# Stick-breaking output by partial summation: suffix products times value differences in place of sigmoid times suffix product

## The chip, the cores and the metric

The program is one inference step of a two-layer encoder trunk. It runs on one core of a Trainium2 chip, as one launch. Such a core has five engines that run side by side, each through its own list of instructions in order: TensorE (PE in the profile, with its weight loads as PEld), VectorE (DVE), ScalarE (ACT), GpSimd (POOL) and SyncE (SP), the last two of which issue most of the DMA transfers here. They wait for each other by semaphores. The metric is the time of the whole launch in microseconds (us): median 2755.19 us of three runs (2753.42 to 2755.53).

## The reference: what is computed

The change touches one thing, the stick-breaking attention of layer 0 for the prompt: 1024 positions, 8 heads of 64 columns, blocks of 128 queries.

```python
def stick_breaking(q, k, v, q_pos, k_pos):
    z = jnp.einsum('bqhd,bkhd->bhqk', q, k).astype(jnp.float32) * (HEAD_DIM ** -0.5)
    mask = k_pos[None, :] < q_pos[:, None]
    log_keep = jnp.where(mask, jax.nn.log_sigmoid(-z), 0.0)
    between = lax.cumsum(log_keep, axis=3, reverse=True) - log_keep
    w = jnp.where(mask, jnp.exp(jax.nn.log_sigmoid(z) + between), 0.0)
    return jnp.einsum('bhqk,bkhd->bqhd', w.astype(v.dtype), v)
```

With keep_k = sigmoid(-z_k) (1 where masked), the weight of key j is sigmoid(z_j) times the product of keep_k over all later keys k > j. Write S_j for the product of keep_k over k >= j. Since sigmoid(z_j) = 1 - keep_j, the weight is also S_{j+1} - S_j, with S_n = 1 behind the last key.

Beside the prompt, layer 0 computes the same for 8 sample streams of 16 queries against 1024 cached and 16 new keys, and a convolution module (31 taps, depthwise, 512 channels) in parallel. An output projection, a squared-ReLU MLP, a second layer with chunk-band attention and a second MLP follow.

## The kernel before

Layer 0's mixer is the function `mixer0`; in the trace it fills the first 545 us or so. Tokens stand along the free dimension, channels on the 128 partitions: 1152 tokens (`T`), 1024 of them prompt (`TP`). The 8 heads go by pairs `p` = 0 to 3, two heads `i` to a pair. Per pair, five lists of steps are merged: the prompt's attention (`attend`), the sample attention, the projections of the next pair (`proj(p+1)`) and, for pairs 0 and 1, the gate and value projections of two further convolution channel blocks (`ag`). The merge goes by the PE time of each step. Into this list come the convolution's taps (`tap`, one DVE operation over 1024 columns and one over 128 for each of 31 taps of each of 4 channel blocks), spread by their DVE cost: 26 ahead of pair 0, then 36, 38 and 24 in pairs 0, 1 and 2. In pair 3 the place of the projections is taken by the first part of the output projection (`psoa`), the convolution's normalisation (`conv_norm`) and the reload of finished pieces from DRAM (`cr`). The program's recording layer then fixes the order of each engine's own list, which can differ from the order of the code by some places.

One head's attention goes in four jobs `t` of two query blocks (`q` = 2t, 2t+1). For a block of n = 128(q+1) keys:

- PE makes the logits z (names `z`, lines 924 to 927), 512 columns to a bank.
- ACT takes sigmoid(z) into `w` (tile `sg`, line 928) and sigmoid(-z) into `keep` (tile `kp`, line 929).
- DVE runs `stick`: a scan from the right that turns `keep` into suffix products (line 907), then w[j] times keep[j+1] (line 909).
- PE transposes w block by block (`tpa`, line 388), ACT copies the transposed blocks out (`wa`, line 390), PE multiplies them by the transposed values `vs` (`ava`, line 398), two half-results on partitions 0 to 63 and 64 to 127 of one bank.
- `finish`: ACT copies one half out (`ata`, line 406), DVE adds the other (`cpa`, line 410), and POOL stores the piece in DRAM (`cat_d`, line 363).

The values of a pair arrive from the projection as tile `sv` (channels by tokens). POOL stores that tile as an output (`out_sb_v`, line 881). `expand_v` transposes it on PE in three groups (`vt`, line 898), and ACT copies the result into `vs` (line 900) and, for the sample's new keys, into `vn` (line 903). The sample attention calls the same `stick` from `soft`, with tiles `sgs` and `kps`.

Tiles with one tag share buffers: `sg` has three, `kp` two, `sv` and `vs` one each.

Of the kernel before, what the change touches and what calls it, by code (L numbers as in the profile page):

```python
# [8 lines left out]
F32 = mybir.dt.float32  # L9
F32R = mybir.dt.float32r  # L10
AF = mybir.ActivationFunctionType
ALU = mybir.AluOpType
# [3 lines left out]
P = 128  # L16
# [3 lines left out]
TP = 1024  # L20
# [104 lines left out]
def tile_trunk(ctx, tc, ins, outs):  # L125
    nc = tc.nc
    ACT = nc.scalar.activation
    tt = nc.vector.tensor_tensor
# [5 lines left out]
    def pool(name):  # L134
        return tc.tile_pool(name=name, bufs=1, reuse_waits="tile")
# [7 lines left out]
    def bank(name):  # L143
        return psum.tile([P, 512], F32, tag="ps", name=name)
# [225 lines left out]
                split(hi, lo, piece[rows, at - c0:at - c0 + m])  # L370
                at += m

    def weigh_steps(vs, wk, cat, i, t, blocks, name, scored):


        order = sorted(blocks.keys, key=lambda j: -len(blocks.keys[j]))
        groups = []
        for two in zip(order[::2], order[1::2]):
            n, m = (P * len(blocks.keys[j]) for j in two)
            groups.append(([(two[0], 0, n), (two[1], n, m)], n + m))  # L380
        st = {"w": {}}

        def turn(gi):
            items, used = groups[gi]
            tp = bank(f"tp{name}{gi}")
            for j, c0, n in items:
                for q, tile_q in enumerate(blocks.keys[j]):
                    nc.tensor.transpose(tp[:, c0 + q * P:c0 + (q + 1) * P], blocks.get(j, tile_q), ident)
            st["w"][gi] = wk.tile([P, 512], F32, tag="wt", name=f"w{name}{gi}")
            ACT(st["w"][gi][:, :used], tp[:, :used], AF.Copy)  # L390

        def prod(gi):

            if gi == 0:
                st["av"] = bank(f"av{name}")
            for m, (j, c0, n) in enumerate(groups[gi][0]):
                o0 = 0 if 2 * t in blocks.keys[j] else P
                mm(st["av"][64 * m:64 * m + 64, o0:o0 + n], vs[:, j, i], st["w"][gi][:, c0:c0 + n], start=gi == 0,
                   stop=gi == last)

        def finish():
            own = slice(64 * i, 64 * i + 64)
            av = st["av"]
            one = P if t == 0 else 0
            tmp = wk.tile([P, 256], F32, tag="av", name=f"at{name}")
            ACT(tmp[own, one:], av[64:128, one:256], AF.Copy)
            piece = wk.tile([P, 256], F32, tag="cat", name=f"cp{name}")
            if one:
                ACT(piece[own, :one], av[0:64, :one], AF.Copy)
            prior["weights"] = tt(piece[own, one:], av[0:64, one:256], tmp[own, one:], ALU.add)  # L410
            cat.put(piece, own, t * 256, 256)

        def pcost(gi):
            return 4 * groups[gi][0][0][2] * PASS

        def tcost(gi):
            return groups[gi][1] / P * 109

        last = len(groups) - 1
        def turns(gi):  # L420
            return Step(tcost(gi), lambda: turn(gi), 0.0, f"turn{name}{gi}", None if gi else scored, 4500)

        lag = 4500 if cat.layer == 0 else 2500

        def prods():
            for gi in range(last + 1):
                prod(gi)
            finish()


        return ([turns(gi) for gi in range(last + 1)]
                + [Step(sum(pcost(gi) for gi in range(last + 1)), prods, 330.0, f"out{name}", f"turn{name}{last}", lag)])
# [222 lines left out]
    def mixer0():  # L655
        with ExitStack() as st:

            ep = Bufs(st.enter_context(pool("early0")), sg=3, kp=2)
# [3 lines left out]
            maskd = ep.tile([P, P], F32R, "maskd", "maskd")  # L662
            unit = ep.tile([P, P], F32R, "unit", "unit")
            rp = Bufs(st.enter_context(pool("rstd0")), rv=3)
            pp = Bufs(st.enter_context(pool("pair0")))
            wk = Bufs(st.enter_context(pool("work0")), wt=4, wts=1, cat=2)
            S = {"qb": qb}

# [216 lines left out]
            def expand_qk(p):  # L885
# [4 lines left out]
                ACT(S["qn"], q[:, TP:], AF.Copy, scale=0.125)  # L890
                ACT(S["kn"], k[:, TP:], AF.Copy)

            def expand_v(p, g):
                v = S["sv", p]
                tp = bank(f"vt0{p}{g}")
                for i in range(3):
                    c = (3 * g + i) * P
                    nc.tensor.transpose(tp[:, i * P:(i + 1) * P], v[:, c:c + P], ident)
                n = 3 if g < 2 else 2
                ACT(vs[:, 3 * g:3 * g + n], tp[:, :n * P].rearrange("p (j h d) -> p j h d", j=n, h=2), AF.Copy)  # L900
                if g == 2:
                    S["vn"] = pp.tile([P, P], F32, "vn", f"vn0{p}")
                    ACT(S["vn"], tp[:, 2 * P:3 * P], AF.Copy)

            def stick(w, keep, n):

                nc.vector.tensor_tensor_scan(keep[:, 0:n][:, ::-1], keep[:, 0:n][:, ::-1],  # L907
                                             ones[:, 0:1].to_broadcast([P, n]), 1.0, ALU.mult, ALU.mult)
                tt(w[:, 0:n - 1], w[:, 0:n - 1], keep[:, 1:n], ALU.mult)

            def attend(p, cat):
                def job(i, t):
                    ws = {}

                    def one(q):
                        n = (q + 1) * P
                        w = ep.tile([P, TP], F32, "sg", f"sg{p}{i}{q}")
                        keep = ep.tile([P, TP + P], F32, "kp", f"kp{p}{i}{q}")
                        qc = slice(q * P, q * P + P)
                        for c in range(0, n, 512):  # L920
                            m = min(512, n - c)
                            z = bank(f"z{p}{i}{q}{c}")
                            last = c + m == n
                            mm(z[:, :m], qs[i][:, qc], kd[i][:, c:c + m], start=True, stop=False)
                            mm(z[:, :m], qs[i][:, qc], kl[i][:, c:c + m], start=False, stop=not last)
                            if last:
                                mm(z[:, m - P:m], unit, maskd, start=False, stop=True)
                            ACT(w[:, c:c + m], z[:, :m], AF.Sigmoid)
                            ACT(keep[:, c:c + m], z[:, :m], AF.Sigmoid, scale=-1.0)
                        stick(w, keep, n)  # L930
                        ws[q] = w

                    keys = {j: [q for q in (2 * t, 2 * t + 1) if j <= q] for j in range(2 * t + 2)}
                    blocks = Blocks(keys, lambda j, q: ws[q][:, j * P:(j + 1) * P])
                    q0, q1 = 2 * t, 2 * t + 1

                    def cost(q):
                        return 2 * max(256, q * P + P) * PASS

                    def dcost(q):  # L940
                        return 2 * (60 + (q * P + P) / 0.96)

                    name = f"a{p}{i}{t}"
                    return (Step(cost(q0), lambda: one(q0), dcost(q0)),
                            Step(cost(q1), lambda: one(q1), dcost(q1), f"z{name}"),
                            weigh_steps(vs, wk, cat, i, t, blocks, name, f"z{name}"))

                return [job(i, t) for i in range(2) for t in range(4)]

            def soft(bg, z, zn, s):  # L950
                tt(zn[:, 0:P], zn[:, 0:P], masks[:, 0, 64 - 64 * bg:192 - 64 * bg], ALU.add)
                w = wk.tile([P, TP + P], F32, "sgs", f"sgs{s['p']}{bg}")
                keep = ep.tile([P, TP + P], F32, "kp", f"kps{s['p']}{bg}")
                for src, c, n in ((zn, TP, P), (z[1], 512, 512), (z[0], 0, 512)):
                    ACT(w[:, c:c + n], src[:, :n], AF.Sigmoid)
                    ACT(keep[:, c:c + n], src[:, :n], AF.Sigmoid, scale=-1.0)
                stick(w, keep, TP + P)
                s["w"] = w

            start()  # L960
# [1 line left out]
            vs = pp.tile([P, 8, 2, HD], F32, "vs", "vs0")  # L962
# [3 lines left out]
            for p in range(4):  # L966
                S["p"] = p
                expand_qk(p)
                if p < 3:
# [3 lines left out]
                    n = TAPS[p + 1]  # L973
# [8 lines left out]
                cat = Cat(0, p, wk, cat_t)  # L982
                jobs = attend(p, cat)
                body, left = pipeline(jobs[1:], jobs[0][2])
                steps = carry + [jobs[0][0]] + [Step(327.0, lambda p=p, g=g: expand_v(p, g)) for g in range(NG)]
                if p == 3:
                    late, = ready_chunks(0, [2], pp, cat_t)
# [750 lines left out]
    class Next:  # L1738
# [48 lines left out]
        def run_rows(self, g):  # L1787
            self.rows[g]()

    cat = mixer0()  # L1790
    rst = Bufs(ctx.enter_context(pool("rstd")), rv=3)
    with pool("mlp0") as mp_:
# [39 lines left out]
    cat = mixer1(n1, win)  # L1832
# [134 lines left out]
```

## Time and profile before

| what | us |
|---|---|
| median of three runs | 2755.19 |
| lowest, highest | 2753.42, 2755.53 |
| span of the profiled execution, first to last instruction | 2748.2 |
| PE busy in it | 2669.0 |
| DVE busy in it | 2090.5 |
| ACT busy in it | 1389.0 |

The profile is of one execution; it has a span of its own, 7.0 us below the median of the timed runs. The page lists for each engine how long it was busy, cuts the span in 40 slices, follows the chain of waits back from the last instruction, and groups instructions by line, operation and tile: the count, the sum of the busy time (overlaps counted once), the mean of one in ns, and the idle time before them with what ended it. Other views used below are tables by stretch of time, lists of one engine's instructions in order of time with the idle time before each in square brackets, and totals of who waited for whom. Matmuls overlap in the pipeline and their ends are modelled, so a busy PE is not PE at its peak; PE's idle time is the sure part.

### The profile page before, as it was taken

How to read it: one execution, taken by the hardware profiler on the slowest of the kernel's cores; microseconds unless marked ns; L12 is line 12 of the kernel's file. 1: busy time of each engine (PE TensorE's matmuls, PEld its weight loads, DVE VectorE, ACT ScalarE, POOL GpSimd, SP SyncE). 2: the span in 40 equal slices, each digit the busy share in tenths (PEclk: the TensorE clock that was granted, in tenths of full speed). 3: DMA queues.
4: the chain of work that ended last, by engine and by line, in shares of the span. 5: the costliest groups of instructions: out<-in, count | busy, mean ns of one | idle time of the engine just before them, and what ended most of it. 6: DMA issues, size and time to landing. Idle time of an engine off the chain costs nothing.

```text
span 2748.2 us, 50583 instructions
## 1 busy us (share of the span) xinstructions
PE 2669.0 (97%) x19362; PEld 2557.1 (93%) x19362; DVE 2090.5 (76%) x4117; ACT 1389.0 (51%) x2906; POOL 328.3 (12%) x599
## 2 busy tenths in 40 slices
PE   8999898999999999999999999998999999999998
PEld 8987776799999999999999999997999999999998
DVE  8999998888777755758577777778787777647577
ACT  5344456755554543435355555556555555434344
POOL 1100101041111100000011111110221111100001
PEclk9999999999999999999999999999999999999999
DMA  4434446454343377435444444446533343684344
GB/s 157 121 111 147 118 141 223 145 176 143 139 146 141 138 260 250 124 100 170 146 140 138 140 135 135 139 132 229 179 132 137 141 145 138 230 270 134 96 125 145
DMA packets 173203, 422.90 MB, mean 154 GB/s; under 512 B 25968, under 2 KB 53808, under 8 KB 170912
## 3 DMA queue, kind: packets, MB, share of 16 engines
q1 hardware_dynamic: 135696, 288.38, 33.1%
q0 software_dynamic: 37120, 131.27, 13.9%
q8 instruction: 152, 2.49, 0.4%
q14 instruction: 91, 0.75, 0.1%
q10 hardware_dynamic: 144, 0.02, 0.0%
HBM read 289.60 MB, written 117.34 MB: 148 GB/s over the span
## 4 chain that ended last, share of the span: by engine, by line
PE 76%; DVE 12%; ACT 4%; issue 4%; DMA 3%; POOL 0%; SPq 0%; DVEq 0%; ACTq 0%; POOLq 0%
PE um L1461 25%; PE pd L1686 25%; PE psc L225 10%; PE psp L225 3%; DVE y L735 3%; PE avc L467 2%; PE tpc L455 2%; DVE kp L907 2%; PE f L225 1%; PE psoa L225 1%; DMA cr<-cat_d 1%; PE zc L1201 1%; PE zc L1202 1%; PE zs L568 1%; PE so L602 1%
## 5 line engine op out<-in xcount | busy, mean ns | idle before, releaser
L225 PE MATMUL psc<-h,hl_wc 128*128 128x384 f32 x1728 | 327.2, 339 | 0.0
L225 PEld LDWEIGHTS psc<-h,hl_wc 128*128 128x128 f32 x1728 | 296.8, 188 | 13.3 <-issue 10.9
L1461 PE MATMUL um<-sl,hl_m 128*128 128x288 f32 x1548 | 240.3, 295 | 0.0
L1461 PEld LDWEIGHTS um<-sl,hl_m 128*128 128x128 f32 x1548 | 217.7, 188 | 0.0
L1686 PE MATMUL pd<-tm,hl_wd 128*128 128x288 f32 x1584 | 214.7, 294 | 0.0
L1686 PEld LDWEIGHTS pd<-tm,hl_wd 128*128 128x128 f32 x1584 | 211.3, 189 | 0.0
L735 DVE SCALAR_TENSOR_TENSOR y<-u,dw,y 128x1024 f32<-128x1024 f32 (+1 forms) x232 | 177.8, 806 | 0.6
L225 PE MATMUL psp<-h,hl_wi 128*128 128x384 f32 x864 | 165.7, 344 | 0.0
L1468 ACT ACTIVATE hdm<-hdm 128x288 f32<-128x288 f32 x192 | 84.7, 442 | 156.5 <-DVE hdm L1467 154.8
L225 PEld LDWEIGHTS psp<-h,hl_wi 128*128 128x128 f32 x864 | 150.9, 191 | 7.0 <-issue 6.2
L186 DVE TENSOR_TENSOR tm<-xr,tm 128x576 fp32r<-128x576 f32 (+1 forms) x120 | 85.8, 715 | 93.9 <-ACT tm L185 93.6
L185 ACT ACTIVATE tm<-xr 128x576 fp32r<-128x576 f32 (+1 forms) x120 | 77.6, 646 | 95.8 <-PE pd L1686 74.0
L1168 ACT ACTIVATE s<-s,mxc 128x640 f32<-128x640 f32 (+4 forms) x128 | 88.9, 694 | 60.2 <-DVE mxc L1165 58.6
L1461 PE MATMUL um<-sl,hl 128*128 128x288 f32 x756 | 119.1, 296 | 0.0
L1686 PE MATMUL pd<-th,hl_wd 128*128 128x288 f32 x792 | 113.7, 297 | 3.8 <-DVE th L186 3.7
L1686 PEld LDWEIGHTS pd<-th,hl_wd 128*128 128x128 f32 x792 | 108.2, 190 | 4.8 <-DVE th L186 4.2
L1686 PE MATMUL pd<-xr,hl_wd 128*128 128x288 f32 x792 | 112.4, 296 | 0.0
L1686 PEld LDWEIGHTS pd<-xr,hl_wd 128*128 128x128 f32 x792 | 108.0, 190 | 0.0
L1461 PEld LDWEIGHTS um<-sl,hl 128*128 128x128 f32 x756 | 106.4, 188 | 0.8
L1686 PE MATMUL pd<-tm,hl 128*128 128x288 f32 x768 | 104.9, 295 | 0.0
L1686 PEld LDWEIGHTS pd<-tm,hl 128*128 128x128 f32 x768 | 103.1, 188 | 0.0
L185 ACT ACTIVATE whc<-tpc 128x512 fp32r<-128x512 f32 (+1 forms) x144 | 72.5, 523 | 46.7 <-PE tpc L455 45.8
(526 smaller groups left out, 6637.0 us busy)
## 6 DMA issues: line engine op xcount, KB each, us to landing
xr<-hb_d SPq DMA_DIRECT2D x208, 288.0 KB, 3.0
xr<-in_w_up_dram SPq DMA_DIRECT2D x64, 512.0 KB, 4.2
hb_d<-hdm POOLq DMA_DIRECT2D x96, 288.0 KB, 2.4
hb_d<-t POOLq DMA_DIRECT2D x96, 288.0 KB, 2.4
wm<-in_w_down_dram SPq DMA_DIRECT2D x64, 256.0 KB, 4.0
st_wd<-in_w_down_dram SPq DMA_DIRECT2D x64, 256.0 KB, 3.5
st_wc<-in_w_in_c_dram SPq DMA_DIRECT2D x44, 256.0 KB, 2.9
xm_d<-xo POOLq DMA_DIRECT2D x16, 576.0 KB, 3.5
```

The source lines that it names most:

```text
L185: ACT(hi, src, AF.Copy)
L186: return tt(lo, src, f(hi), ALU.subtract)
L225: mm(ps()[:, :G], hl[:, a, at:at + P], act[g][k // 4][b][:, k % 4, :], start=n == 0, stop=n == len(todo) - 1)
L455: nc.tensor.transpose(tp[:, c0 + q * P:c0 + (q + 1) * P], blocks.get(j, tile_q), ident)
L467: mm(st["av"][:, o0:o0 + n], vs[:, j, i].rearrange("p a d -> p (a d)"), src[:, c0:c0 + n], start=st["done"] == 0, stop=st["done"] == nmm - 1)
L568: mm(box["z"][at // 512][own, at % 512:at % 512 + kw], qb[:, own], k[:, b * kw:b * kw + kw], start=True, stop=True)
L735: stt(src if j == CW - 1 else dst, src, wj, dst, ALU.mult, ALU.add)
L907: nc.vector.tensor_tensor_scan(keep[:, 0:n][:, ::-1], keep[:, 0:n][:, ::-1], ones[:, 0:1].to_broadcast([P, n]), 1.0, ALU.mult, ALU.mult)
L1168: ACT(s[:, :n], s[:, :n], AF.Exp, bias=mx, scale=-1.0, accum_out=tot)
L1461: mm(banks[b, n][:, :TQ], w[:, a, c * P:c * P + P], combo(key, c)[:, h, n * TQ:n * TQ + TQ], start=k < 3 and c == 0 and i == 0, stop=c == ...
L1468: ACT(y, y, AF.Relu)
L1686: mm(ps, w[:, a, m * P:m * P + P], b[:, h, (n - ns[0]) * TQ:(n - ns[0]) * TQ + TQ], start=first and s == 0, stop=j == NJ - 1 and s == 2, s ...
```

## The change

`stick` keeps the scan and loses the product. For the prompt, only sigmoid(-z) is taken, into tile `sg`; its suffix products S go straight to the transposes. The values are replaced by differences: column j of `sv` becomes v[j-1] - v[j], column 0 becomes -v[0] (the new function `differences`, called ahead of the transposes of each pair, once the values have been sent to the output). Then the sum over j of S_j (v[j-1] - v[j]) plus the value of the block's last key is the output. That last value, for the 8 query blocks of a head, is copied ahead into a small tile `ve`, on both halves of the partitions, and comes in as the bias of the copy in `finish`, which is made once per query block since each has a bias of its own. The sample attention keeps both sigmoids and the product, which moves from `stick` into `soft`.

```diff
-    def weigh_steps(vs, wk, cat, i, t, blocks, name, scored):
+    def weigh_steps(vs, ends, wk, cat, i, t, blocks, name, scored):
...
             tmp = wk.tile([P, 256], F32, tag="av", name=f"at{name}")
-            ACT(tmp[own, one:], av[64:128, one:256], AF.Copy)
             piece = wk.tile([P, 256], F32, tag="cat", name=f"cp{name}")
-            if one:
-                ACT(piece[own, :one], av[0:64, :one], AF.Copy)
+
+            for e in range(2):
+                cols = slice(e * P, e * P + P)
+                dst, rows = (piece, slice(0, 64)) if one and e == 0 else (tmp, slice(64, 128))
+                ACT(dst[own, cols], av[rows, cols], AF.Identity, bias=ends()[rows, i, 2 * t + e:2 * t + e + 1])
             prior["weights"] = tt(piece[own, one:], av[0:64, one:256], tmp[own, one:], ALU.add)
...
-            pp = Bufs(st.enter_context(pool("pair0")))
+            pp = Bufs(st.enter_context(pool("pair0")), ve=2)
...
+            def differences(p):
+
+
+                v = S["sv", p]
+                ends = S["ends", p] = pp.tile([P, 2, 8], F32, "ve", f"ve{p}")
+                for i in range(2):
+                    for rows in (slice(0, 64), slice(64, 128)):
+                        ACT(ends[rows, i], v[64 * i:64 * i + 64, P - 1:TP:P], AF.Copy)
+                tt(v[:, 1:TP][:, ::-1], v[:, 0:TP - 1][:, ::-1], v[:, 1:TP][:, ::-1], ALU.subtract)
+                ACT(v[:, 0:1], v[:, 0:1], AF.Copy, scale=-1.0)
+
             def expand_v(p, g):
                 v = S["sv", p]
+                if g == 0:
+                    differences(p)
...
-            def stick(w, keep, n):
+            def stick(keep, n):
 
                 nc.vector.tensor_tensor_scan(keep[:, 0:n][:, ::-1], keep[:, 0:n][:, ::-1],
                                              ones[:, 0:1].to_broadcast([P, n]), 1.0, ALU.mult, ALU.mult)
-                tt(w[:, 0:n - 1], w[:, 0:n - 1], keep[:, 1:n], ALU.mult)
...
-                        w = ep.tile([P, TP], F32, "sg", f"sg{p}{i}{q}")
-                        keep = ep.tile([P, TP + P], F32, "kp", f"kp{p}{i}{q}")
+                        keep = ep.tile([P, TP], F32, "sg", f"sg{p}{i}{q}")
...
-                            ACT(w[:, c:c + m], z[:, :m], AF.Sigmoid)
                             ACT(keep[:, c:c + m], z[:, :m], AF.Sigmoid, scale=-1.0)
-                        stick(w, keep, n)
-                        ws[q] = w
+                        stick(keep, n)
+                        ws[q] = keep
...
-                stick(w, keep, TP + P)
+                stick(keep, TP + P)
+                tt(w[:, 0:TP + P - 1], w[:, 0:TP + P - 1], keep[:, 1:TP + P], ALU.mult)
```

The order of the engines' lists moves with it at three places that matter below. In these lists the number behind a name is its buffer, and the scan is listed as SCALAR_TENSOR_TENSOR with `ones` as input. Lines 735, 877, 907, 924 and 925 of before are 737, 879, 922, 937 and 938 of the changed kernel.

First, DVE at the start of pair 0, behind the first block's scan (`y` are convolution taps). Before:

```order
L907 SCALAR_TENSOR_TENSOR kp_1099<-kp_1099,ones 128x128
L735 SCALAR_TENSOR_TENSOR y_771<-u_382,dw,y_771 128x1024
L909 TENSOR_TENSOR sg_1098<-sg_1098,kp_1099 128x127
L735 SCALAR_TENSOR_TENSOR y_771<-u_382,dw,y_771 128x1024
L735 SCALAR_TENSOR_TENSOR y_771<-u_382,dw,y_771 128x128
L735 SCALAR_TENSOR_TENSOR y_771<-u_382,dw,y_771 128x1024
L877 TENSOR_TENSOR sq_1178<-psp_1108,rh_315 128x384
```

and of the changed kernel, at the same place:

```order
L922 SCALAR_TENSOR_TENSOR sg_1098<-sg_1098,ones 128x128
L737 SCALAR_TENSOR_TENSOR y_771<-u_382,dw,y_771 128x1024
L737 SCALAR_TENSOR_TENSOR y_771<-u_382,dw,y_771 128x128
L737 SCALAR_TENSOR_TENSOR y_771<-u_382,dw,y_771 128x1024
L903 TENSOR_TENSOR sv_1003<-sv_1003 128x1023
L737 SCALAR_TENSOR_TENSOR y_771<-u_382,dw,y_771 128x1024
L879 TENSOR_TENSOR sq_1179<-psp_1105,rh_315 128x384
```

The product is gone, and three tap operations behind the scan stands the difference of the values, which waits for the transfer of `sv` to the output.

Second, PE at the same time (`psp` is the next pair's projection, `vt` the transposes of the values). Before, the transposes stood between the halves of a group of the projection:

```order
L225 MATMUL psp_1108<-h_30_171,hl_wi_0_966 128x384
L898 MATMUL vt_1121<-ident,sv_1003 128x128 x3
L898 MATMUL vt_1128<-ident,sv_1003 128x128 x3
L898 MATMUL vt_1133<-ident,sv_1003 128x128 x3
L568 MATMUL zs_1140<-ct00k_1142,qb_124 32x256 x4
L225 MATMUL psp_1108<-h_40_178,hl_wi_1_971 128x384
```

Now they stand behind the second half, ahead of the second block's logits:

```order
L225 MATMUL psp_1105<-h_70_190,hl_wi_1_971 128x384
L913 MATMUL vt_1125<-ident,sv_1003 128x128 x3
L913 MATMUL vt_1132<-ident,sv_1003 128x128 x3
L913 MATMUL vt_1137<-ident,sv_1003 128x128 x3
L570 MATMUL zs_1144<-ct00k_1146,qb_124 32x256 x4
L937 MATMUL z_1173<-k_743,q_741 128x256
```

They moved down by 12 matmuls of 384 columns, and behind them PE can do nothing else while they wait.

Third, DVE at the end of pair 0, where the last block's weights are made while pair 1 is prepared (`l` and `q` are the split keys and queries of the next pair, `u` the last tap). Before:

```order
L735 SCALAR_TENSOR_TENSOR u_389<-u_389,dw,y_1239 128x1024
L735 SCALAR_TENSOR_TENSOR u_389<-u_389,dw,y_1239 128x8x16
L351 TENSOR_TENSOR l_745<-sk_1870,k_743 64x1024
L907 SCALAR_TENSOR_TENSOR kp_2126<-kp_2126,ones 128x1024
L351 TENSOR_TENSOR l_746<-sk_1870,k_744 64x1024
L909 TENSOR_TENSOR sg_2125<-sg_2125,kp_2126 128x1023
```

Now:

```order
L737 SCALAR_TENSOR_TENSOR u_389<-u_389,dw,y_1237 128x1024
L922 SCALAR_TENSOR_TENSOR sg_2084<-sg_2084,ones 128x1024
L737 SCALAR_TENSOR_TENSOR u_389<-u_389,dw,y_1237 128x8x16
L351 TENSOR_TENSOR l_746<-sk_1840,k_744 64x1024
L353 SCALAR_TENSOR_TENSOR q_742<-sq_1179,q_742 64x1024
```

The scan, now the last step ahead of PE's transposes, stands ahead of the split keys instead of between them. In pairs 1 and 2 the differences stand among the next convolution block's taps, more than 20 operations behind DVE's last part of the values; in pair 3 they stand 17 behind it, after the split of the first reloaded piece.

More of the change, by code (lines that the diff above doesn't have):

```diff
@@ L945, in job @@
                             Step(cost(q1), lambda: one(q1), dcost(q1), f"z{name}"),
[L946 removed]
+                            weigh_steps(vs, lambda: S["ends", p], wk, cat, i, t, blocks, name, f"z{name}"))
                 return [job(i, t) for i in range(2) for t in range(4)]
```

## Prediction

> **What bounds the kernel now.** I first asked which engine is full where the changed work stands. A table by stretches of the trace, with the attention's pairs 0 to 2 in the first (100 to 425 us), the change to pair 3 in the second and pair 3 in the third, gives per stretch its length and each engine's busy time with its count, then the clock and the DMA engines:
>
> ```profile
> core 0: us, PE busy (x) PEld busy (x) DVE busy (x) ACT busy (x) POOL busy (x), PEclk, DMA share, GB/s
> 225.00:250.00 25.00, 25.00 (x176) 20.51 (x174) 23.33 (x35) 10.59 (x28) 0.54 (x1) 1.00 0.41 128
> 275.00:300.00 25.00, 22.46 (x173) 19.50 (x172) 22.85 (x33) 11.15 (x29) 2.50 (x4) 1.00 0.28 72
> 100.00:425.00 325.00, 305.26 (x2276) 261.34 (x2274) 316.97 (x418) 160.78 (x376) 31.61 (x56) 0.98 0.44 132
> 425.00:445.00 20.00, 12.53 (x64) 7.84 (x65) 10.84 (x18) 6.89 (x15) 4.88 (x10) 0.83 0.90 303
> 445.00:550.00 105.00, 98.44 (x718) 78.96 (x715) 94.17 (x177) 84.84 (x186) 8.69 (x16) 0.98 0.51 172
> ```
>
> From 100 to 425 us DVE is busy 316.97 of 325 (97.5%), PE 305.26. Two engines are nearly full, and PE's 19.7 us of idle time are all that can certainly be had while PE's work stays as it is. Whom it waits for is told by the totals of PE's waits in that stretch (us in total, times, longest):
>
> ```profile
> PE tpa L388 <- DVE sg L909: 16.1, 7, 6.2
> PE z L924 <- DVE u L715: 1.0, 1, 1.0
> PE tpa L388 <- DVE cpa L410: 0.8, 1, 0.8
> PE z L924 <- DVE sk L877: 0.7, 1, 0.7
> ```
>
> 18.6 of the 19.7 us are waits for DVE, 16.1 of them of the transposes for the very product that goes. So DVE decides here, though PE looks full. How DVE comes to be late is seen at the longest wait, in DVE's and PE's lists in order of time (start, duration; idle time before it in brackets):
>
> ```profile
> 205.32 5.91 DVE L735 SCALAR_TENSOR_TENSOR y<-u,dw,y 128x128 f32<-128x128 f32 x8
> ...
> 214.47 2.27 DVE L907 TENSOR_TENSOR_SCAN kp<-kp,ones 128x1024 f32<-128x1024 f32 x1
> 216.78 1.22 DVE L351 TENSOR_TENSOR l<-sk,k 64x1024 fp32r<-64x1024 f32 x1
> 218.03 1.23 DVE L909 TENSOR_TENSOR sg<-sg,kp 128x1023 f32<-128x1023 f32 x1
> 219.31 0.90 PE L388 MATMUL tpa<-ident,sg 128*128 128x128 f32 x3 [6.17 <-DVE sg L909]
> ```
>
> PE stops at 213.1. DVE works on without a gap, taps first, starts the last block's scan 1.3 us later and ends its product at 219.3: a backlog, not one slow operation. Such a wait costs twice. The table of PE in steps of 2 us (busy time, then the granted clock) shows the clock at half from 216 to 222 us, past the wait's end:
>
> ```profile
> 212.00:214.00 2.00, 1.14 (x7) 1.00 0.00 0
> 214.00:216.00 2.00, 0.00 (x0) 0.80 0.65 262
> ...
> 220.00:222.00 2.00, 2.00 (x8) 0.50 0.66 128
> 222.00:224.00 2.00, 2.00 (x20) 0.99 0.91 218
> ```
>
> From 219.3 to 222 PE worked at half speed, which lost 1.35 us more.
>
> **The change part by part.** The groups that go, and the nearest rows for what is added:
>
> ```profile
> L909 DVE TENSOR_TENSOR sg<-sg,kp 128x127 f32<-128x127 f32 (+3 forms) x64 | 47.9, 749 | 0.6
> L928 ACT ACTIVATE sg<-z 128x512 f32<-128x512 f32 (+2 forms) x96 | 47.8, 498 | 19.8 <-PE z L927 10.1 <-PE tpa L388 4.6 <-PE z L925 4.1
> L406 ACT ACTIVATE ata<-ava 64x256 f32<-64x256 f32 (+1 forms) x32 | 11.3, 354 | 41.1 <-PE ava L398 40.7
> L1041 ACT ACTIVATE yl<-yl,cvec 128x384 f32<-128x384 f32 x12 | 8.2, 697 | 0.1
> L1773 ACT ACTIVATE sqh<-x 128x384 f32<-128x384 f32 x21 | 9.6, 512 | 0.7 <-DVE accs L1774 0.5
> ```
>
> *DVE.* 64 products go, 47.9 us. Four subtractions of 128x1023 come; their row is the product of that size, 1.23 us at 218.03: 4.9 us. Net 43.0, of which pairs 0 to 2 hold three quarters, 32.3. DVE's work in the first stretch falls to 284.7 us.
>
> *ACT.* 96 sigmoids go, 47.8 us. The copies of `finish` become two of 128 columns with a bias, in place of one of 256. An operation of 128x384 with two operands read per partition took 697 ns against 512 without (L1041, L1773), so about 0.09 us for one; 0.27 us is the shortest L406 copy, of 128 columns. That makes 2 x 0.36 in place of 0.38, or +0.34 us for each of 24 jobs and +0.18 for each of 8: 9.6 us. The four copies of last values and the sign change cost at most 5 x 0.27 per pair, 5.4. Net 33 us less. ACT is busy half of the first stretch, so I count none of this as gain; the 0.34 us in `finish` lie under other PE work, and without that cover would be 32 x 0.34 = 11 us at most.
>
> *PE* does the same matmuls.
>
> *What follows for PE, pairs 0 to 2.* The 18.6 us of waits for DVE shrink but needn't vanish: DVE's 284.7 us will stand in about 309, still 92%. The table's slices where DVE is as busy today, 225 to 250 (93%) and 275 to 300 (91%), have 0 and 2.54 us of PE idle. That bounds the rest by 0 and 309/25 x 2.54 = 31, which is more than today; between such ends I go by the longest waits, which are a backlog of 3 to 6 us built up over 100 us of stretch, when a pair now frees 10.8 us of DVE. I leave 5.0 us. Gain 13.6, and 1.35 for the clock.
>
> *The new wait.* `sv` may be overwritten only when its store has landed; then DVE subtracts, ACT changes a sign, and PE transposes. In pair 0 there is no distance:
>
> ```profile
> 106.97 0.56 POOL L881 DMA_DIRECT2D out_sb_v_dram<-sv  x1 [3.93 <-ACT sv L879]
> out_sb_v_dram<-sv POOLq DMA_DIRECT2D x1, 576.0 KB, 4.0
> out_sb_v_dram<-sv POOLq DMA_DIRECT2D x1, 576.0 KB, 9.2
> 106.27 2.34 PE L225 MATMUL psp<-h,hl_wi 128*128 128x384 f32 x12
> 108.44 1.15 PE L898 MATMUL vt<-ident,sv 128*128 128x128 f32 x9
> 108.99 0.41 DVE L907 TENSOR_TENSOR_SCAN kp<-kp,ones 128x128 f32<-128x128 f32 x1
> 109.32 1.25 DVE L735 SCALAR_TENSOR_TENSOR y<-u,dw,y 128x1024 f32<-128x1024 f32 x1
> ```
>
> The store is issued at 107.0 and took 4.0 us to land (pair 0; 9.2 in pair 3): 111.0. DVE's list puts a scan and three tap operations from 109.0 ahead of the subtraction, to 112.0. Plus 1.23 and some 0.4 for ACT and two signals: 113.6. PE, with 12 more matmuls ahead (2.1 us), is there at 110.5. So PE stands 3.1 us, and behind its transposes queue all later logits and projections; DVE fills its own time with taps. For a clock that may drop in it I add 0.7, half of the 1.35 above. In pairs 1 to 3 the subtraction stands 17 or more DVE operations behind the last of the values, and PE's transposes later still: nothing, as long as a store lands within about 10 us. Cost 3.8.
>
> [...]
>
> *Into pair 3.* The chain of waits goes through reloaded pieces (`cr`), the first of which may start when DVE has split the last keys (line 351):
>
> ```profile
> 419.08 1.05 ACT L348 ACTIVATE k<-sk 64x1024 fp32r<-64x1024 f32 x1 [0.17 <-PE z L924]
> 423.56 1.22 DVE L351 TENSOR_TENSOR l<-sk,k 64x1024 fp32r<-64x1024 f32 x1
> 424.81 7.86 DMA cr<-cat_d
> 434.77 6.57 DMA cr<-cat_d
> ```
>
> The keys were ready at 420.1, DVE came at 423.56. PE idles 7.5 us from 425 to 445, but two transfers of 7.86 and 6.57 us stand in a row behind that split, so this stretch gains only DVE's lateness: 3.4.
>
> *Pair 3.* PE's waits there for DVE or for a `keep` tile, from the totals of 445 to 550:
>
> ```profile
> PE sn L582 <- DVE cpa L410: 1.2, 1, 1.2
> PE st L588 <- ACT kp L929: 1.0, 1, 1.0
> PE z L924 <- DVE cs L638: 0.7, 1, 0.7
> PE st L588 <- DVE xo L1086: 0.7, 1, 0.7
> PE tpa L388 <- DVE xo L1086: 0.4, 1, 0.4
> ```
>
> Together 4.0 us. Here no subtraction is left to pay, and 12 us of DVE's 94 go; I count them whole. Behind 550 us nothing is touched.
>
> *Sum.* 13.6 + 1.35 - 3.8 + 3.4 + 4.0 = 18.5 us. The profiled span goes from 2748.2 to 2729.7. The timed median lies 7.0 us above the span; carried over, 2755.2 - 18.5 = **2737 us**.
>
> **The rivals.** *Waits stay (2747).* In-order lists, taps first: the backlog forms again, 13 us of the 18.6 stay, and the gain in pair 3 halves. 5.6 + 1.35 - 3.8 + 3.4 + 2.0 = 8.5 us. For it speaks the slice with 91% and 2.5 us idle; against it that 16.1 us hang on the removed product itself.
>
> *DVE sets the pace outright (2721).* PE's busy time is partly modelled; its weight loads are busy only 261.34 of 325 us. If PE has hidden room, the first stretch shortens by DVE's whole 32.3 us less the 3.8: 28.5, with 3.4 and part of pair 3 (2.5) 34.4. Against it: PE's list shows nearly unbroken matmuls, and small ones need little loading. [...]
>
> *Nothing to be seen (2754).* Residual waits of 15 us and half the gain behind: 3.6 + 1.35 - 3.8 + 0 = about 1.
>
> *Slower (2768).* The wait for the store, in every pair. DVE's list is in order: should the store land late (9.2 us instead of 4.0 would move 113.6 to 117.8), DVE, the sign change on ACT and all of PE stand behind it. 7.3 us and 1.4 of clock per pair make 34.8; without any such wait the gain would be 22.3, so 12.5 lost. It decides from 22.3/4 = 5.6 us per pair. Against it: the distance in pairs 1 to 3.
>
> **How the numbers follow.** Forecast 0.54, waits stay 0.17, DVE's pace 0.11, nothing 0.11, slower 0.07. Two runs of this kernel can't tell less than 0.2% (5.5 us) from no change: faster is the first three, 0.82, same 0.11, slower 0.07. The forecast's own range is 2731 to 2744 (residual waits of 0 to 11 us give 2732 to 2743, pair 0's wait of 0 to 7 gives 2733 to 2741, one at a time). To leave out no more than 2 in 10 the range takes in the stay of waits and most of DVE's pace: 2721 to 2752.
>
> **What would show it.** Right: no wait of `tpa` above 2 us between 100 and 425, DVE's share there near 92%, a wait of `vt` of about 3 us near 110, the first `cr` earlier by more than the rest, the later stages unchanged in length. Wrong: PE's waits of the same total on another DVE row (`cpa`, `u`), waits for `sv` in pairs 1 to 3, or a stretch that shortens by more than PE's idle time.

## The result, and the profile after

The changed kernel takes 2728.57 us (median of four runs, 2724.97 to 2731.01) against 2754.31 us before (four runs, 2749.01 to 2755.53): ratio 0.991, 95% interval 0.9896 to 0.9924. The forecast was 2737 us, faster. The profiled execution spans 2727.3 us, 20.9 us less than that of before.

To see where the 20.9 us lie, both traces are cut at the same events: the first transposes of the values (`vt`) of pairs 0, 1, 2 and 3, and the first `psob` matmul (second part of the output projection), which ends pair 3. The fifth row is everything from the first MLP on. The columns are the stretch and its length, each engine's busy time (operations), the mean granted clock, the DMA share and GB/s. Before:

```profile
core 0: us, PE busy (x) PEld busy (x) DVE busy (x) ACT busy (x) POOL busy (x), PEclk, DMA share, GB/s
108.44:234.33 125.89, 117.58 (x866) 100.94 (x865) 121.91 (x164) 56.05 (x128) 12.23 (x22) 0.97 0.48 143
234.33:349.03 114.70, 107.75 (x795) 92.11 (x795) 111.79 (x150) 55.45 (x130) 10.98 (x19) 0.99 0.42 127
349.03:447.13 98.10, 86.15 (x653) 68.85 (x653) 87.39 (x116) 55.39 (x132) 12.21 (x22) 0.95 0.49 157
447.13:542.66 95.53, 89.09 (x658) 71.10 (x657) 86.17 (x161) 77.31 (x170) 8.69 (x16) 0.98 0.53 182
605.83:2748.20 2142.37, 2106.58 (x15495) 2065.23 (x15494) 1536.99 (x3272) 1055.89 (x2180) 244.94 (x458) 1.00 0.48 155
```

After:

```profile
111.32:226.97 115.65, 113.51 (x854) 97.83 (x854) 109.10 (x144) 50.37 (x116) 12.45 (x22) 1.00 0.49 147
226.97:333.96 106.99, 105.35 (x794) 90.87 (x794) 102.34 (x135) 48.93 (x117) 11.43 (x19) 1.00 0.44 137
333.96:425.67 91.71, 84.39 (x651) 67.83 (x652) 77.81 (x102) 50.11 (x120) 12.23 (x22) 0.94 0.53 167
425.67:518.27 92.60, 86.97 (x658) 69.64 (x657) 76.09 (x144) 70.08 (x150) 8.68 (x16) 1.00 0.56 188
581.83:2727.30 2145.47, 2109.58 (x15495) 2068.16 (x15494) 1536.49 (x3272) 1056.39 (x2181) 245.73 (x458) 0.99 0.46 155
```

Pairs 0 to 3 are shorter by 10.2, 7.7, 6.4 and 2.9 us. Their start is 2.9 us later, the output projection 0.4 and the rest of the program 3.1 us longer. The 3.1 us are not the change's: the trace's records of the granted clock show 27.2 us at half speed there against 20.8 before, on the same instructions. Nor is it the change's that PE's first logits (`z`), behind the same 528 matmuls, start at 103.75 us instead of 105.98: of these 2.2 us up to 1.7 (half of 3.41) are a half speed from 51.4 to 54.8 us, which of the two only the trace of before has. In pair 0, 12 matmuls (866 less 854) are not saved but moved ahead of the cut, some 2.1 us.

The waits of PE from 100 to 409 us (us in total, times, longest), pairs 0 to 2 of the changed kernel, answer to the totals shown of before, where `tpa` for `sg` alone had 16.1 us, longest 6.2:

```profile
PE vt L913 <- ACT sv L904: 4.6, 2, 2.9
PE tpa L388 <- DVE sg L922: 4.3, 3, 2.5
```

In PE's list in order of time these three waits stand at the ends of pairs 0, 1 and 2:

```profile
210.38 0.55 PE L388 MATMUL tpa<-ident,sg 128*128 128x128 f32 x3 [0.16 <-DVE sg L922]
321.20 0.98 PE L388 MATMUL tpa<-ident,sg 128*128 128x128 f32 x7 [1.57 <-DVE sg L922]
405.70 1.14 PE L388 MATMUL tpa<-ident,sg 128*128 128x128 f32 x7 [2.52 <-DVE sg L922]
```

The 6.17 us at 219.31 have become 0.16. The new waits, for the differences (store, subtraction, sign change, transposes; first in pair 0, then in pair 1):

```profile
104.74 0.56 POOL L883 DMA_DIRECT2D out_sb_v_dram<-sv  x1 [3.93 <-ACT sv L881]
107.09 2.72 DVE L737 SCALAR_TENSOR_TENSOR y<-u,dw,y 128x1024 f32<-128x1024 f32 x3
109.72 1.22 DVE L903 TENSOR_TENSOR sv<-sv 128x1023 f32<-128x1023 f32 x1
110.97 0.20 ACT L904 ACTIVATE sv<-sv 128x1 f32<-128x1 f32 x1 [5.05 <-DVE sv L903]
111.32 1.17 PE L913 MATMUL vt<-ident,sv 128*128 128x128 f32 x9 [2.87 <-ACT sv L904]
...
221.09 4.45 DVE L737 SCALAR_TENSOR_TENSOR y<-u,dw,y 128x1024 f32<-128x1024 f32 x6
225.47 1.21 DVE L903 TENSOR_TENSOR sv<-sv 128x1023 f32<-128x1023 f32 x1
226.97 0.55 PE L913 MATMUL vt<-ident,sv 128*128 128x128 f32 x3 [1.78 <-ACT sv L904]
```

In pair 0 PE waits 2.87 us, in pair 1 1.78 us. The store was issued at 104.74 and took 4.0 us, so it had landed at 108.7, and DVE came to the subtraction only at 109.72, straight out of three taps; in pair 1 too it comes straight out of a row of taps. So both waits are for DVE's turn. In none of the four pairs was DVE idle ahead of the subtraction, so none of them waited for the store.

### The profile page after: what moved, and what is told of

Its sections match the earlier page's. It is cut to its first block, busy times and chain, and to the rows that moved or that the text cites. A ratio compares the mean times of both kernels' runs of the same rounds, so it can differ in the third digit from the quotient of the medians.

```text
span 2727.3 us, 50453 instructions
## 1 busy us (share of the span) xinstructions
PE 2662.2 (98%) x19362; PEld 2553.9 (94%) x19362; DVE 2053.9 (75%) x4057; ACT 1366.1 (50%) x2854; POOL 330.2 (12%) x599
## 4 chain that ended last, share of the span: by engine, by line
PE 70%; DVE 5%; ACT 2%; DMA 1%; issue 1%; DVEq 0%; ACTq 0%; SPq 0%
PE pd L1699 25%; PE um L1474 25%; PE psc L225 10%; PE avc L469 2%; PE tpc L457 2%; PE zc L1214 1%; PE zc L1215 1%; PE psoa L225 1%; PE so L604 1%; PE zs L570 1%; DVE xr L1380 0%; PE psob L225 0%; DMA cr<-cat_d 0%; ACT s L1181 0%; DVE sl L1704 0%
```

## The experiments

"The change again" is a second profile and five more runs of the changed kernel. Line numbers shift by some lines from kernel to kernel. Lengths of pairs and waits are of one profiled execution each, times in us are medians of 4 to 10 runs. Each ratio is to runs of before on the same chip, whose medians lay between 2751.38 and 2752.69 us.

**Which part brings it.** The first kernel is before with the product left out of the prompt's attention and nothing else: both sigmoids stay, and the suffix products go to the transposes in place of the weights, so the weights' last step is not computed.

```diff
-            def stick(w, keep, n):
+            def stick(w, keep, n, product=True):
...
-                tt(w[:, 0:n - 1], w[:, 0:n - 1], keep[:, 1:n], ALU.mult)
+                if product:
+                    tt(w[:, 0:n - 1], w[:, 0:n - 1], keep[:, 1:n], ALU.mult)
...
-                        stick(w, keep, n)
-                        ws[q] = w
+                        stick(w, keep, n, False)
+                        ws[q] = keep
```

(`keep` takes the tag `sg` and `w` the tag `kp`.)

> The kernel before with the product alone left out for the prompt: both sigmoids are taken as before, the suffix products go to the transposes, the values stay undifferenced, so the output of the prompt's attention is not the reference's. Backlog theory (VectorE's time decides): all of the 47.9 us of products go and no new wait comes, so as fast as the change or a few us faster, 2723 to 2731. ScalarE theory (the sigmoid that goes decides): near the kernel before, 2748 to 2756. Latency theory (the product stood between scan and transposes): like the backlog theory.

Measured: 2734.67 us, ratio 0.9935 (0.9913 to 0.9958), 18 us less than before, but some 4 us above the range expected by the backlog theory. Its pair 3, in the columns of the tables above:

```profile
427.29:523.56 96.27, 90.06 (x658) 71.93 (x657) 76.08 (x144) 77.78 (x170) 8.67 (x16) 0.96 0.54 180
```

Pairs 0 to 2 have 115.5, 107.4 and 95.7 us, so the product alone brings 20.1 of the 24.3 us there, and it moves no matmuls and adds no wait ahead of them; what is left of PE's waits for the suffix products is 3.7 us in all, against 4.3 in the changed kernel. But pair 3 has gained nothing (95.5 before), although DVE has 10 us less to do in it; 6.8 us at half clock in place of 3.4 are up to 1.7 us of that.

Next, the changed kernel with the sigmoid that it dropped, into a tile that nobody reads:

```diff
+                        w = ep.tile([P, TP + P], F32, "kp", f"kp{p}{i}{q}")
...
+                            ACT(w[:, c:c + m], z[:, :m], AF.Sigmoid)
                             ACT(keep[:, c:c + m], z[:, :m], AF.Sigmoid, scale=-1.0)
```

> The changed kernel with the second sigmoid taken again into a tile that nobody reads: ScalarE has its 47.8 us back. Backlog and latency theories: the time of the changed kernel, 2725 to 2733. ScalarE theory: most of the gain is lost, 2742 or more.

Measured: 2739.58 us, ratio 0.9959 (0.9945 to 0.9973), between the two expectations. ACT's time, which the prediction counted as no gain, is worth about 11 us. The next two give DVE its product back instead: once beside the path, into a tile nobody reads, and once in it, as a multiplication of the suffix products by one ahead of the transposes.

```diff
+                        w = ep.tile([P, TP + P], F32, "kp", f"kp{p}{i}{q}")
...
                         stick(keep, n)
+                        tt(w[:, 0:n - 1], keep[:, 0:n - 1], keep[:, 1:n], ALU.mult)
```

> The changed kernel with a product of the same size on VectorE behind each scan, into a tile that nobody reads: VectorE's 47.9 us are back, but nothing waits for them. Backlog theory: PE's waits for the suffix products and the half clock come back, 2745 to 2757 (with the differences on top perhaps above the kernel before). Latency and ScalarE theories: the time of the changed kernel, 2725 to 2735.

```diff
                         stick(keep, n)
+                        tt(keep[:, 0:n - 1], keep[:, 0:n - 1], ones[:, 0:1].to_broadcast([P, n - 1]), ALU.mult)
```

> The changed kernel with the suffix products multiplied by one in place behind each scan: VectorE's time is back and the transposes wait for it. Backlog theory: no more than 1.2 us per visible wait above the run with the product beside the path, 2746 to 2760. Latency theory: this one alone is slow, 2745 to 2757, and the one beside the path is not. ScalarE theory: 2725 to 2735.

Measured: beside the path 2756.81 us, ratio 1.0021 (1.0011 to 1.0031); in it 2757.36 us, ratio 1.0019 (1.0008 to 1.0029). The whole gain is gone in both, and the product costs the same whether PE waits for it or not. So what counted was DVE's time, as a backlog, and not one more step between the scan and the transposes. The waits of PE up to 720 us with the product beside the path show how: the transposes wait for the scan itself, which stands behind products that nobody needs.

```profile
PE tpa L388 <- DVE sg L922: 12.4, 4, 4.6
PE vt L913 <- ACT sv L904: 8.1, 3, 4.7
```

**The wait for the store.** The differences go to a tile of their own, so that they need not wait until the store of the values has landed:

```diff
-                tt(v[:, 1:TP][:, ::-1], v[:, 0:TP - 1][:, ::-1], v[:, 1:TP][:, ::-1], ALU.subtract)
-                ACT(v[:, 0:1], v[:, 0:1], AF.Copy, scale=-1.0)
+                d = S["sd", p] = ep.tile([P, TP + P], F32, "kp", f"sd{p}")
+                tt(d[:, 1:TP], v[:, 0:TP - 1], v[:, 1:TP], ALU.subtract)
+                ACT(d[:, 0:1], v[:, 0:1], AF.Copy, scale=-1.0)
...
-                    nc.tensor.transpose(tp[:, i * P:(i + 1) * P], v[:, c:c + P], ident)
+                    nc.tensor.transpose(tp[:, i * P:(i + 1) * P], (S["sd", p] if c < TP else v)[:, c:c + P], ident)
```

> The changed kernel with the differences written into a tile of their own (tag kp, whose two buffers the prompt no longer uses), so that nothing waits for the store of the values. Theory that the new wait costs its 2.9 + 1.8 us of PE idle time in pairs 0 and 1: 4 to 5 us faster than the changed kernel in the same call. Rival, that the time is taken up by later waits (the reloaded pieces at the start of pair 3): less than 2 us.

Measured: 2727.44 us, ratio 0.9905 (0.9891 to 0.9919), against 2728.77 us for the change again beside it: 1.3 us, which these runs cannot tell from nothing, and not the 4 to 5 us expected. PE's waits in pairs 0 and 1:

```profile
110.17 1.07 PE L914 MATMUL vt<-ident,sd 128*128 128x128 f32 x8 [0.85 <-DVE sd L904]
226.53 0.52 PE L914 MATMUL vt<-ident,sd 128*128 128x128 f32 x3 [1.63 <-DVE sd L904]
```

In pair 0 2.0 of the 2.87 us are gone, in pair 1 hardly anything. Since the changed kernel did not wait for the store either, what went in pair 0 is a matter of DVE's list: in this kernel the subtraction stands right behind the first block's scan (starts at 108.82 and 108.49 us), and the taps that stood ahead of it (2.72 us) stand behind it. That the list was made so because no store has to land first is likely, but is not shown.

**Pair 3.** Three kernels put one piece back in part of the pairs: the sigmoid in pair 3 only, the sigmoid in pairs 0 to 2 only, and the product beside the path in pair 3 only. The edits are those above, under `if p == 3` or `if p < 3`. With them ran the changed kernel itself.

> The changed kernel once more, as the mark for the other runs of this call: 24 to 27 us below the kernel before by every theory; the theory that phases of the clock are chance lets its parts move by some us each.

> The changed kernel with the second sigmoid back in pair 3 only, into a tile that nobody reads. Theory that ScalarE decides in pair 3 alone (81% busy there before): as slow as with the sigmoid back everywhere, 8 to 13 us above the changed kernel. Rival, a loss spread over the pairs: a quarter of that, 2 to 4 us.

> The changed kernel with the second sigmoid back in pairs 0 to 2 only. Theory that ScalarE decides in pair 3 alone: the time of the changed kernel within 2 us. Rival, a loss spread over the pairs: 6 to 9 us above it.

> The changed kernel with a product of the same size beside the path, as in the run with it everywhere, but in pair 3 only: VectorE has 12 us back there. Theory that both engines are near their limit in pair 3: 4 to 8 us above the changed kernel. Rival, that ScalarE alone decides there: within 2 us of it.

| kernel | us | ratio (95%) | pair 3, us |
|---|---|---|---|
| the change again | 2728.77 | 0.9919 (0.9904 to 0.9935) | 93.05 |
| sigmoid back in pair 3 | 2738.94 | 0.9957 (0.9941 to 0.9973) | 100.85 |
| sigmoid back in pairs 0 to 2 | 2732.82 | 0.9932 (0.9917 to 0.9947) | 93.05 |
| product beside in pair 3 | 2735.31 | 0.9943 (0.9929 to 0.9958) | 98.65 |

The change again lies 22.9 us below before, where 24 to 27 were expected. The product in pair 3 costs 6.5 us, as expected if both engines are near their limit there. The rows of pair 3: the change again, the sigmoid back there, the product back there.

```profile
425.77:518.82 93.05, 88.46 (x659) 70.90 (x658) 76.30 (x144) 70.10 (x150) 8.69 (x16) 0.98 0.55 187
```

```profile
426.06:526.91 100.85, 94.17 (x659) 74.89 (x658) 77.03 (x144) 79.50 (x175) 8.68 (x16) 0.92 0.52 172
```

```profile
425.79:524.44 98.65, 91.27 (x659) 72.42 (x658) 86.53 (x161) 71.39 (x152) 8.69 (x16) 0.97 0.53 176
```

9.4 us more of ACT in pair 3 lengthen it by 7.8, and 10.2 us more of DVE by 5.6: in this pair both engines stand close behind PE. (Both lengths are above the 95.5 us of before, which has both pieces. Part of that is the clock, at half for 17.1 and 6.8 us in place of 3.4; the rest stays open.) In pairs 0 to 2 the same sigmoid costs nothing in pairs 0 and 1 (115.7 and 107.0 us, unchanged) and 1.6 us in pair 2. By the timed runs the sigmoid costs 10.2 us in pair 3, as expected if ACT decides there, and 4.0 us in pairs 0 to 2, between the two expectations and with intervals that overlap. Whether it costs by ACT's backlog, or because a bank of logits is held for two sigmoids in place of one, these runs don't separate. With the sigmoid back, PE's idle time in pair 3 rises by only 2.1 us (4.6 to 6.7); its busy time rises by 5.7, because the clock stands at half for 17.1 us in place of 3.4. What stands ahead of such a record is seen in the kernel with the sigmoid back there, in three steps of 3.41 us, the length of the shortest records of half clock, laid so that the last begins, to within 0.13 us, where the record of half clock begins:

```profile
489.00:492.40 3.40, 2.33 (x16) 1.75 (x14) 3.40 (x9) 3.14 (x7) 0.55 (x2) 1.00 0.59 174
492.40:495.81 3.41, 1.79 (x9) 1.13 (x9) 2.62 (x7) 3.26 (x8) 1.07 (x2) 0.98 0.87 291
495.81:499.22 3.41, 2.77 (x8) 2.46 (x9) 2.04 (x3) 3.41 (x10) 0.00 (x0) 0.50 0.11 40
```

No wait within them is longer than 1.2 us, but in the middle step PE worked only 1.79 us, and from its end the clock is recorded at 0.50.

**Towards a faster version.** Three edits to the changed kernel, each on something that the rows above showed. In pair 3, one copy without a bias and the last value added by DVE, which spares ACT:

```diff
+            late = cat.p == 3
+            if late:
+                ACT(tmp[own, one:], av[64:128, one:256], AF.Copy)
...
+                    prior["weights"] = stt(piece[own, cols], av[0:64, cols], ends()[own, i, 2 * t + e:2 * t + e + 1],
+                                           tmp[own, cols], ALU.add, ALU.add)
```

> The changed kernel with, in pair 3 only, one plain copy of 256 columns on ScalarE and the last value added by VectorE with the sum (two operations of 128 columns there). Theory that ScalarE decides in pair 3: its 8 x 0.34 = 2.7 us less there shorten pair 3 by 1 to 4 us. Theory that VectorE decides there: 0 to 2 us longer.

The first two reloaded pieces in the buffers of `kp`, which the prompt's blocks no longer use, so that they need not wait for the keys' split:

```diff
-                cr = pp.tile([P, T], F32, "sk", f"cr{layer}{c}")
+                cr = pp.tile([P, T], F32, "kp" if layer == 0 and c < 2 else "sk", f"cr{layer}{c}")
...
-                    fill = ready_chunks(0, range(2), pp, cat_t) + first + [late] + fill
+                    fill = ready_chunks(0, range(2), ep, cat_t) + first + [late] + fill
```

> The changed kernel with the first two reloaded pieces in the two kp buffers, so that they no longer wait for VectorE's split of the last keys nor for each other. Theory that the two transfers in a row hold PE at the start of pair 3: the wait of psoa for cat (4.3 us) and the half clock around it (10.2 us of half speed) go, 5 to 9 us below the changed kernel (2728.6 to 2728.8): 2719 to 2724. Rival, that PE waits for the same time on something else there: less than 2 us.

And both together with the differences' own tile in pairs 0 to 2:

> The changed kernel with the reload ahead, the bias on VectorE in pair 3 and, in pairs 0 to 2, the differences in a tile of their own: the sum of the gains of the single runs, 7 to 13 us below the changed kernel (2716 to 2722), or, if the gains lie in the same time, that of the reload alone.

Measured: bias on DVE 2731.45 us, ratio 0.9928 (0.9914 to 0.9943); reload ahead 2729.01 us, 0.9911 (0.9892 to 0.993); all three 2723.37 us, 0.9897 (0.9882 to 0.9911). The first changes nothing that can be told: pair 3 has 93.8 us, where 1 to 4 us less were expected if ACT decides there. The second is above the 2719 to 2724 us expected. It does what it says in pair 2, whose end is the way into pair 3 (changed kernel 91.71 us, 84.39 busy). First reload ahead, then all three:

```profile
340.36:427.19 86.83, 83.09 (x652) 67.64 (x652) 77.82 (x101) 49.74 (x120) 12.23 (x22) 0.98 0.57 176
```

```profile
333.72:420.87 87.15, 81.94 (x653) 66.16 (x653) 77.72 (x101) 49.56 (x120) 12.23 (x22) 1.00 0.56 176
```

That is 4.9 and 4.6 us less. In the profile of the reload alone they were given back in pairs 0 and 1 (118.4 and 108.5 us in place of 115.7 and 107.0), where that edit changes no operation and DVE's list is the same, at half clock (6.1 and 3.4 us by the records). The kernel with the bias on DVE shows the same (118.40 and 108.51 us). So it was the clock, and the same wait at the start of pair 0 shows where these profiles part from that of the changed kernel. PE waits 2.87 us for the differences in the changed kernel, 2.88 us in the one with the bias on DVE:

```profile
111.22 2.15 PE L922 MATMUL vt<-ident,sv 128*128 128x128 f32 x9 [2.88 <-ACT sv L913]
```

Steps of 3.41 us, laid in the same way by the records of the clock, around that wait; first the changed kernel, then this one:

```profile
106.13:109.54 3.41, 2.32 (x14) 2.00 (x12) 3.41 (x6) 0.00 (x0) 0.00 (x0) 1.00 0.85 303
109.54:112.95 3.41, 1.63 (x17) 1.12 (x17) 3.41 (x5) 1.28 (x5) 0.00 (x0) 1.00 0.00 0
```

```profile
107.25:110.66 3.41, 1.09 (x7) 0.77 (x5) 3.41 (x4) 0.00 (x0) 0.00 (x0) 0.99 0.54 184
110.66:114.07 3.41, 2.85 (x17) 1.99 (x17) 3.03 (x4) 1.74 (x5) 0.00 (x0) 0.50 0.00 0
```

In the one the wait is cut in two by a step's border and no step is left with less than 1.63 us of work; in the other it lies almost whole in one step, 1.09 us of work remain in it, the clock of the next is 0.50, and the transposes that took 1.17 us take 2.15.

All three edits together give the fastest kernel of the study, about 5 us under the change (7 to 13 were expected), but the two intervals overlap a little. That the reload is shorter is shown; how much of the 5 us are its, and how much the luck of the clock, stays open.

## Why the prediction was right, and where it was off

The sign and the main mechanism were right, and the sum was 18.5 us for 20.9 in the profile. That it came so near is partly luck: up to the start of pair 3 the profile gained 21.5 us where 14.55 were counted, of which 2.2 lie ahead of the pairs and are not the change's, and 3.1 us were lost again to the clock in the part that the change doesn't touch. Term by term, by that sum's own steps:

- **DVE's work.** 32.3 us less were expected in pairs 0 to 2; the tables give 321.1 less 289.3, 31.8. The rows of the groups (busy, mean ns) up to 620 us give the added operations as they were priced, 0.36 and 1.23 us:

```profile
L411 ACT ACTIVATE ata<-ava,ve 64x128 f32<-64x128 f32 x56 | 17.8, 359 | 26.3 <-PE ava L398 19.9 <-DVE y L737 6.0
L903 DVE TENSOR_TENSOR sv<-sv 128x1023 f32<-128x1023 f32 x4 | 4.9, 1213 | 0.0
```

- **ACT's work.** 33 us less were expected; in the tables of pairs 0 to 3 it is 24.7 (244.2 less 219.5). No term of the sum hangs on it.
- **PE's waits.** 18.6 less 5.0 us, less 3.1 of new wait, plus 3.4 on the way into pair 3: 13.9 us less idle expected in pairs 0 to 2. Measured 27.2 less 11.1 in the tables, less the 2.87 ahead of them: 13.2. The waits for the suffix products left are 4.3 us. The rival with waits that stay (13 us of them) is refuted. DVE's share is 92.0% of pairs 0 to 2 (289.3 of 314.4 us), as forecast; one wait of 2.52 us is above the 2 us set as the sign.
- **The clock, mis-sized.** This is the step that failed most. The sum took 1.35 us for one stretch at half speed and 0.7 back. In pairs 0 to 2 PE's busy time fell by 8.2 us, of which the 12 moved matmuls are 2.1; 6.1 remain where 0.65 stood. The records show 20.5 us at half clock before in these pairs and 10.2 after, by estimate worth up to 5.1 us, half of the difference; the rest I cannot place. One stretch was read in detail, and the other low values of the clock in the same stage were not priced. Nor is the wait of 6.17 us, read in the prediction, the only one with half the clock behind it. In the trace of before the clock is at half from 406.4 to 409.8 us behind the wait of 1.74 us shown here, and from 307.4 to 310.8 us behind one of 1.64 us.

```profile
405.44 0.84 PE L388 MATMUL tpa<-ident,sg 128*128 128x128 f32 x6 [1.74 <-DVE sg L909]
```

- **The new wait.** 3.1 us expected in pair 0, 2.87 found. As the prediction had it, DVE's list and not the store came last there; the 1.23 us and some 0.4 counted behind it were 1.22 and 0.38 (subtraction from 109.72, `vt` at 111.32). "Nothing" in pair 1 was wrong by 1.78 us, and such a wait was named as a sign of being wrong: the subtraction's many operations of distance on DVE protect it from the store, not from DVE's own lateness. The 0.7 us for the clock is in truth nothing or, as in two of the experiments, 2.7 us (115.7 to 118.4).
- **Into pair 3: 3.4 us expected, nothing gained.** The rows that answer to the keys and their split in the prediction:

```profile
397.53 1.06 ACT L348 ACTIVATE k<-sk 64x1024 fp32r<-64x1024 f32 x1 [0.17 <-PE z L937]
400.84 1.22 DVE L351 TENSOR_TENSOR l<-sk,k 64x1024 fp32r<-64x1024 f32 x1
```

The keys were ready at 398.6 and DVE came 2.25 us later, so only 1.2 of its 3.4 us of lateness went. The first reload took 8.50 us in place of 7.86, and the half clock there is 10.2 us in place of 6.8. From the keys to the first transposes of pair 3 it is 27.1 us, as before (27.0), so all that was gained up to there lies ahead of the keys. The stretch itself was rightly seen as bound by the reload: PE's longest wait there, from 409 to 429 us, is still

```profile
PE psoa L225 <- ACT cat L185: 4.6, 2, 4.3
```

With the reload ahead there is no wait on that row between 405 and 430 us.
- **Pair 3, right number and wrong reason.** 4.0 us of PE's waits were expected to go, all by DVE; 2.9 came, but PE's idle time fell by only 0.8 (6.4 to 5.6), and up to 1.7 are the clock, which in this profile was nowhere at half there (3.4 us before). In the second profile, with as much half clock as before, 2.5 us came. The product alone brings nothing that can be told there, and the changed kernel with ACT's sigmoid put back is 5.3 us longer in pair 3 than before (100.85 to 95.53). By these profiles it takes both. "I count none of this as gain" was argued from ACT's half-busy first stretch and holds there; pair 3, where the quoted row had ACT at 84.84 of 105 us, should have been asked by itself.
- **From the span to the median.** The 7.0 us carried over were mostly chance: the profiled runs of the study lie 1.7 to 2.1 us above their own spans, so the profiled execution of before took about 2750 us, some 5 less than the median of the runs shown. This, and not the sum, makes most of the 8.4 us between 2737 and 2728.57: the span forecast was 2729.7 for 2727.3.
- **Rivals.** DVE as the only pace (2721) fell too, though the time lies between it and the forecast: of 31.8 us freed in pairs 0 to 2, 19.4 came (24.3 in the tables, less 2.1 moved and the 2.87 of wait ahead of pair 0). DVE was the right engine to name; as the only bound it would have given the whole 31.8. That small matmuls need little loading holds in the trace of before: from 100 to 425 us the 192 weight loads of 128x32 of `zs` were busy 4.0 us, the 682 of 128x128 of `psp` 119.3. The slower rival, the wait for the store in every pair, came in none.
- **The signs.** DVE's share, the wait of `vt` and the first `cr` (22.7 us earlier, from 424.8 to 402.1, for 21.5 at the start of pair 3) are as forecast; one `tpa` wait above 2 us and the wait for `sv` in pair 1 are not, nor are the later stages the same in length (0.4 and 3.1 us longer).

## What to carry to other kernels

An engine that works through fillers in order makes another late by its backlog, so what counts is its total time, not which operation stands next to the wait: a useless product cost as much as a needed one (2756.81 and 2757.36 us). Ask each stage which engines stand close behind the bound; one that is half idle on average can bind in one stage (ACT, 50% busy over the changed kernel's span, where its sigmoid put back in pair 3 cost 10.2 us), and where two engines stand close, as in pair 3 here, a change that frees one may gain little until the other is freed too. Price a wait of TensorE with the clock that may fall behind it (nothing or 2.7 us in pair 0 here, behind waits of 2.87 and 2.88 us), and compare two kernels by several runs, since one profile of the same kernel differs from the next by as much as a small change is worth (4.7 us here).

## What the runs showed of the hardware

In the traces of before and of the changed kernel the records of half clock are 3.41, 6.83 or 10.24 us long, but for the last, which runs past the program's end. Within each of the two all of them begin, to 0.004 us, on one grid of 3.413 us. From trace to trace that grid stands elsewhere against the program: at the wait for the differences in pair 0 a border lies near 109.4 us in the changed kernel and near 110.6 in the one with the bias on DVE.

Half the clock was recorded behind steps of the grid in which PE had still worked 1.09 or 1.79 us; behind one with 1.63 us it was not, so the limit isn't sharp in the modelled busy time. Nine traces of this case, cut into such steps (before and the changed kernel from 11 to 2700 us, seven of the experiments from 11 to about 635), say the same: of the steps at full clock, all 18 with under 1.4 us of PE work were followed by half the clock, 22 of the 69 with 1.4 to 2.2 us, and 4 of the 2690 with more.

The same kernel varies by the clock. The changed kernel again spans 2722.6 us, 4.7 less than the first time, and nearly all of it lies in the part that the change doesn't touch:

```profile
582.35:2722.60 2140.25, 2103.11 (x15495) 2061.36 (x15494) 1536.43 (x3272) 1055.77 (x2180) 244.49 (x457) 1.00 0.48 155
```

2140.25 us in place of 2145.47, at 11.9 us of half clock in place of 27.2.
